# First feed-forward chunk computed token-major, weight tile by weight tile

## The chip, the core and the metric

The kernel runs on one core of a Trainium2 chip. Its time is the device time of one execution in microseconds (us). TensorE (PE) multiplies matrices and transposes, VectorE (DVE) and ScalarE (ACT) work element by element, GpSimd (POOL) does small scalar work, and the queue of SyncE (SP) issues the DMAs. PEld is TensorE's weight load.

## The reference

A two-layer decoder trunk over 256 tokens of width 1024, in float32. A layer is a gated feed-forward part, a token mixer (layer 0 a windowed attention beside a stick-breaking one, layer 1 a dilated attention), a cross-attention into 256 memory tokens, and a second feed-forward part. The change lies in the first feed-forward part of layer 0, with which the program begins:

```python
def swiglu_ffn(x, w_gu, w_down):
    gate, up = jnp.split(x @ w_gu, 2, axis=-1)
    return (jax.nn.silu(gate) * up) @ w_down
x = x + 0.5 * swiglu_ffn(rms_norm(x, ffn1_norm[layer]), ffn1_w_gu[layer], ffn1_w_down[layer])
```

`w_gu` is 1024 x 5632 (gate and up, 2816 columns each), `w_down` 2816 x 1024.

## The kernel before, in words

Every float32 operand of a product is split into two parts: a high part rounded to the format fp32r (a copy on ScalarE) and a low part, what is left (a subtraction on VectorE). A product is then three matmuls: high by high, high by low, low by high (`mm3`, lines 181 to 183). A weight tile is 128 x 1024; `weights` (line 166) loads it into one of four "raw" buffers, makes the high part `wh` (line 174) and the low part `wl` (line 176). There are ten buffers of each of these.

The 2816 hidden features are worked in 11 chunks of 256. A chunk needs 1024 rows of 256 gate and 256 up columns: four weight tiles (`load_chunk`, line 352). The normalised x stands transposed, as 8 blocks of 128 features for each of two token tiles (t = 0, 1) of 128 tokens, in `xs` (high and low). Two forms of a chunk exist:

- feature-major: the weights are the stationary operand, x the moving one, and the result has features on the partitions, as the down projection wants it. `ws_wide` (line 309) does it with matmuls of 512 and 256 columns and sums the two halves; `ws_blocks` (line 293) does it with 256-column matmuls of `mm3`, or pass by pass (`by_pass`, line 300).
- token-major: a block of x is stationary, 512 weight columns (256 gate, 256 up) move, 24 matmuls for a token tile. The result has tokens on the partitions; after silu and product (lines 379 and 380) two transposes (line 385) and a split turn it to features.

In the other three feed-forward parts chunks 0 and 1 are token-major and chunks 2 to 10 go through `ws_wide`. In the first part, before the change, chunk 0 goes through `ws_blocks` with its own tiles (four blocks of 1024 rows x 256 columns, two for gate, two for up), and chunks 1 to 10 through `ws_wide`.

The program starts with `start` (line 327). The gain vector of the first norm, a row in memory, is spread over the partitions by a matmul of ones (line 333). For each token tile `x_updated` makes the square sums (ScalarE, line 213) and `norm_T` the reciprocal root (GpSimd, lines 219 to 222), the scaled x (VectorE, line 226), four transposes for each half (line 207) and the split into `xs` (lines 189 and 190). Then the weight tiles of chunk 0 are split.

What sets the order: the Tile planner orders each engine's instructions by when their operands are ready in its own model of the time, and among ready ones takes the one that stands first in the program. In `start`, `tc.manual_schedule` makes GpSimd, VectorE, ScalarE and TensorE keep the written order of the region's instructions among themselves; SyncE's queue, and where instructions from outside the region fall between them, stay with the planner. `later(delay, fn)` puts work off by a written clock that `tick` advances; `need(tag)` does all that is put off under a tag at once. `announce` (line 232) fetches the norm vector of the next part as a broadcast (line 194) and is called at chunk 2 of the first part.

Of the kernel before, what the change touches and what calls it, by code (L numbers as in the profile page):

```python
# [11 lines left out]
F32 = mybir.dt.float32  # L12
# [26 lines left out]
def kernel(  # L39
# [63 lines left out]
    def tick(ns):  # L103
        clock[0] += ns
        if heap and not busy[0] and heap[0][0] <= clock[0]:
            dispatch()
# [19 lines left out]
    nc.sync.dma_start(row[0:1, :], first_vec.rearrange("(o n) -> o n", o=1))  # L126
    ones = wk.tile([P, 512], F32, name="wk")
    nc.gpsimd.memset(ones[0:1, 0:P], 1.0)
    for t in range(2):
        for c in range(2):  # L130
            cs = slice(c * 512, (c + 1) * 512)
            nc.sync.dma_start(xres[t][:, cs], x_in[0, t * P:(t + 1) * P, cs])
    ident = const.tile([P, P], F32, name="ident")
    make_identity(nc, ident)
    ident_b = const.tile([P, P], BF16, name="ident_b")
# [11 lines left out]
    def psum():  # L147
        return mm.tile([P, 512], F32, name="mm")

    def tps():  # L150
        return tp.tile([P, 512], F32, name="tp")
# [10 lines left out]
    def blocks(ap, n=P):  # L162
        return ap.rearrange("p (a b) -> p a b", b=n)


    def weights(src):
        r = raw.tile([P, 1024], F32, name="raw")
        if len(src.shape) == 4:
            for g in range(2):
                nc.sync.dma_start(r.rearrange("p (k g n) -> p k g n", g=2, n=src.shape[3])[:, :, g, :], src[:, :, g, :])  # L170
        else:
            nc.sync.dma_start(r if len(src.shape) == 2 else blocks(r, src.shape[2]), src)
        wh = wsp.tile([P, 1024], F32R, name="wh")
        nc.scalar.copy(wh, r)  # L174
        wl = wsp.tile([P, 1024], F32R, name="wl")
        nc.vector.tensor_tensor(wl, r, f32(wh), op=ALU.subtract)  # L176
        return wh, wl

    def mm3(ps, a, b, start, stop):

# [21 lines left out]

    def transpose4(src):

        ps = psum() if upcoming.get("starting") else tps()
        for b in range(4):
            nc.tensor.transpose(ps[:, b * P:(b + 1) * P], src[:, b * P:(b + 1) * P], ident)  # L207
        tick(440)
        return ps
# [48 lines left out]
    def xboth(k):  # L258
        return xh[:, :, k, :], xl[:, :, k, :]
# [30 lines left out]
                step(1, c, k, ws[k - head])  # L290
            evac(1, c, ps[1][c])

    def ws_blocks(ps, w, off, per, by_pass=False):

        for b in range(2):
            if by_pass:
                for i, (x, y) in enumerate(((0, 0), (1, 0), (0, 1))):
                    for k in range(NK):
                        o = (k % per) * (1024 // per) + off + b * P
                        nc.tensor.matmul(ps[:, b * 256:(b + 1) * 256], lhsT=w[k // per][x][:, o:o + P],  # L300
                                         rhs=xboth(k)[y], start=i == 0 and k == 0, stop=i == 2 and k == NK - 1)
                        tick(110)
                continue
            for k in range(NK):
                o = (k % per) * (1024 // per) + off + b * P
                mm3(ps[:, b * 256:(b + 1) * 256], cols(w[k // per], o, P), xboth(k), k == 0, k == NK - 1)
                tick(330)
# [16 lines left out]
        return out  # L324


    def start(load):

        et = mybir.EngineType
        with tc.manual_schedule(engines={et.Pool, et.DVE, et.Activation, et.PE}):  # L330
            upcoming["gain"] = [psum(), psum()]
            for c in range(2):
                nc.tensor.matmul(upcoming["gain"][c], lhsT=ones[0:1, 0:P], rhs=row[0:1, c * 512:(c + 1) * 512],
                                 start=True, stop=True)
            for t in range(2):
                for c in range(2):
                    x_updated(t, c)
                clock[0] += 3000.0
            upcoming["starting"] = True
            need("x0")  # L340
            first = load(0)
            need("x1")
            rest = load(1)
            upcoming["starting"] = False
            return first, rest

    def ffn(w_gu, w_down, next_vec, first=False):
        wv = w_gu.rearrange("(k p) n -> p k n", p=P)
        wgu = w_gu.rearrange("(k p) (g n) -> p k g n", p=P, g=2)
        hts = []  # L350

        def load_chunk(c):

            return [weights(wgu[:, 2 * i:2 * i + 2, :, c * 256:(c + 1) * 256]) for i in range(4)]

        def hslot(c):
            if c % 2 == 0:
                hts.append((slot(F32R), slot(F32R)))
            return [blocks(h[:, (c % 2) * 512:(c % 2) * 512 + 512], 256) for h in hts[c // 2]]

        ws = hs = None
        if first:
            f, r = start(lambda i: [weights(wv[:, 0:4, 0:256])] if i == 0 else
                         [weights(wv[:, 4 * (n % 2):4 * (n % 2) + 4, (n // 2) * DFF:(n // 2) * DFF + 256])
                          for n in range(1, 4)])
            ws = [[[f[0], r[0]], r[1:]]]
        else:
            need("x0")
            ws = [load_chunk(0), load_chunk(1)]
            hs = [hslot(0), hslot(1)]  # L370
        for t in range(2):
            need(f"x{t}")
            for c in range(0 if first else 2):
                ps = psum()
                for k in range(NK):
                    mm3(ps, xparts(t, k), cols(ws[c][k // 2], (k % 2) * 512, 512), k == 0, k == NK - 1)
                    tick(650)
                h = work()
                nc.scalar.activation(h[:, 0:256], ps[:, 0:256], AF.Silu)
                nc.vector.tensor_tensor(h[:, 256:512], ps[:, 256:512], h[:, 0:256], op=ALU.mult)  # L380

                def to_features(t=t, c=c, h=h):
                    pst = tps()
                    for b in range(2):
                        nc.tensor.transpose(pst[:, b * P:(b + 1) * P], h[:, 256 + b * P:256 + (b + 1) * P], ident)
                    split_to(hs[c][0][:, :, t * P:(t + 1) * P], hs[c][1][:, :, t * P:(t + 1) * P],
                             blocks(pst[:, 0:256]))
                later(LAG['silu'], to_features)
        if not first:
            announce(next_vec)  # L390
        for c in range(0 if first else 2, NF // 2):
            w = ws[0] if first and c == 0 else load_chunk(c)
            if first and c == 2:
                announce(next_vec)
            if first and c == 0:
                pg = psum()
                ws_blocks(pg, w[0], 0, 4, by_pass=True)
                pu = psum()
                ws_blocks(pu, w[1], 0, 4)
            else:  # L400
                pg = ws_wide(w, 0)
                pu = ws_wide(w, 1)
            s = work()
            nc.scalar.activation(s, pg, AF.Silu)
            h = work()
            nc.vector.tensor_tensor(h, pu, s, op=ALU.mult)
            dh, dl = hslot(c)
            split_to(dh, dl, blocks(h, 256))
        flush()

        def hparts(t, k):
            o = (k % 4) * 256 + t * P
            return hts[k // 4][0][:, o:o + P], hts[k // 4][1][:, o:o + P]

        project(lambda k: w_down[k * P:(k + 1) * P, :], hparts, add_to_x(0.5), nk=NF)
# [101 lines left out]
        return evac  # L517


    def even_mixer(w_in, q_gain, k_gain, sinks, w_out, next_vec, mem, first=False):  # L520
        g = gain_col(q_gain, k_gain, 1, 8.0)
        sink = sm.tile([P, 8], F32, name="sink")
        nc.sync.dma_start(sink, sinks.partition_broadcast(P))
# [90 lines left out]

        nsink = sm.tile([P, 8], F32, name="nsink")
        nc.vector.tensor_scalar(nsink, sink, -1.0, None, op0=ALU.mult)
        if first:
            start(lambda i: None)
        need("x0")
        vb = blocks(slot(), 512)  # L620
        wvb = []
# [321 lines left out]
    for i, (layer, part, _) in enumerate(plan):  # L943
        j = layer // 2
        nxt = plan[i + 1][2][plan[i + 1][0]] if i + 1 < len(plan) else None
        mem = mems[layer]
        cross = (layer, 2) in [p[:2] for p in plan]
        if part == 0:
            ffn(ffn1_w_gu[layer], ffn1_w_down[layer], nxt, first=i == 0)
        elif part == 1 and layer % 2 == 0:  # L950
            even_mixer(ev_w_in[j], ev_q_gain[j], ev_k_gain[j], ev_sinks[j], ev_w_out[j], nxt, mem, first=i == 0)
        elif part == 1:
            odd_mixer(od_w_in[j], od_q_gain[j], od_k_gain[j], od_w_out[j], nxt, mem)
        elif part == 2:
            cross_attention(xa_w_q[layer], xa_q_gain[layer], xa_k_gain[layer], xa_w_o[layer], nxt, mem)
        else:
            ffn(ffn2_w_gu[layer], ffn2_w_down[layer], nxt)
# [56 lines left out]
```

## Time and profile before

| | us |
|---|---|
| median of 3 runs | 1220.24 (1218.81 to 1221.25) |
| the profiled execution | 1220.4 |
| its span, first to last instruction | 1218.6 |
| TensorE busy | 1209.0 (99%) |
| weight load busy | 1023.5 (84%) |
| VectorE busy | 762.2 (63%) |
| ScalarE busy | 648.1 (53%) |
| GpSimd busy | 63.8 (5%) |

All times in rows are microseconds from the span's start. A busy TensorE is not one at its peak: matmuls overlap, and their ends are modelled, so the distance from one start to the next tells the pace. In square brackets stands how long the engine was idle before, and what ended that.

### The profile page before, as it was taken

How to read it: one execution, taken by the hardware profiler on the slowest of the kernel's cores; microseconds unless marked ns; L12 is line 12 of the kernel's file. 1: busy time of each engine (PE TensorE's matmuls, PEld its weight loads, DVE VectorE, ACT ScalarE, POOL GpSimd, SP SyncE). 2: the span in 40 equal slices, each digit the busy share in tenths (PEclk: the TensorE clock that was granted, in tenths of full speed). 3: DMA queues.
4: the chain of work that ended last, by engine and by line, in shares of the span. 5: the costliest groups of instructions: out<-in, count | busy, mean ns of one | idle time of the engine just before them, and what ended most of it. 6: DMA issues, size and time to landing. Idle time of an engine off the chain costs nothing.

```text
span 1218.6 us, 17064 instructions
## 1 busy us (share of the span) xinstructions
PE 1209.0 (99%) x6390; PEld 1023.5 (84%) x6390; DVE 762.2 (63%) x979; ACT 648.1 (53%) x1078; POOL 63.8 (5%) x123
## 2 busy tenths in 40 slices
PE   8999999999999999999999999999999999999998
PEld 7888888887888888888888888888788888888887
DVE  6666645665766676665376675376666776667651
ACT  6656534646655565555365554265643654656540
POOL 1000000200010000000000000033000100000000
PEclk9999999999999999999999999999999999999999
DMA  8765664731444485666385657346634545665560
GB/s 261 248 193 176 220 210 136 257 107 35 138 161 143 141 272 171 195 207 207 104 259 174 207 191 263 117 155 202 204 113 139 189 145 158 222 202 178 182 199 35
DMA packets 136756, 216.71 MB, mean 178 GB/s; under 512 B 10337, under 2 KB 104161, under 8 KB 136674
## 3 DMA queue, kind: packets, MB, share of 16 engines
q1 hardware_dynamic: 136674, 215.63, 54.5%
q8 instruction: 50, 0.82, 0.3%
q14 instruction: 32, 0.26, 0.1%
HBM read 214.54 MB, written 1.05 MB: 177 GB/s over the span
## 4 chain that ended last, share of the span: by engine, by line
PE 95%; DVE 1%; DMA 1%; ACT 1%; issue 0%; POOL 0%; SPq 0%; ACTq 0%; POOLq 0%; DVEq 0%
PE mm L318 22%; PE mm L181 18%; PE mm L182 17%; PE mm L183 17%; PE mm L319 12%; PE tp L207 3%; PE mm L800 1%; DMA raw<-in_xa_w_o_dram 1%; PE mm L821 1%; DVE wl L176 1%; PE mm L582 1%; PE mm L300 1%; DMA x<-in_x_dram 0%; PE mm L603 0%; PE mm L680 0%
## 5 line engine op out<-in xcount | busy, mean ns | idle before, releaser
L176 DVE TENSOR_TENSOR wl<-raw,wh 128x1024 fp32r<-128x1024 f32 x386 | 463.7, 1220 | 145.2 <-ACT wh L174 143.8
L174 ACT CAST wh<-raw 128x1024 fp32r<-128x1024 f32 x386 | 394.0, 1051 | 156.2 <-PE mm L183 80.0
L318 PE MATMUL mm<-xs,wh 128*128 128x512 f32 x1184 | 413.7, 394 | 0.0
L319 PE MATMUL mm<-xs,wl 128*128 128x256 f32 x1184 | 331.8, 280 | 0.0
L318 PEld LDWEIGHTS mm<-xs,wh 128*128 128x128 f32 x1184 | 221.8, 187 | 50.4
L319 PEld LDWEIGHTS mm<-xs,wl 128*128 128x128 f32 x1184 | 223.8, 189 | 0.0
L181 PE MATMUL mm<-wh,big 128*128 128x512 f32 x480 | 193.3, 403 | 0.0
L183 PE MATMUL mm<-wh,big 128*128 128x512 f32 x480 | 187.4, 390 | 0.0
L182 PE MATMUL mm<-wl,big 128*128 128x512 f32 x480 | 187.3, 390 | 0.0
L181 PE MATMUL mm<-wh,xs 128*128 128x512 f32 (+1 forms) x432 | 171.9, 398 | 0.0
L182 PE MATMUL mm<-wl,xs 128*128 128x512 f32 (+1 forms) x432 | 167.6, 388 | 0.0
L183 PE MATMUL mm<-wh,xs 128*128 128x512 f32 (+1 forms) x432 | 167.3, 387 | 0.0
L322 ACT COPY wk<-mm 128x256 f32<-128x256 f32 x148 | 55.3, 374 | 152.0 <-PE mm L319 151.6
L323 DVE TENSOR_TENSOR wk<-mm,wk 128x256 f32<-128x256 f32 x148 | 62.3, 421 | 96.9 <-ACT wk L322 96.9
L181 PEld LDWEIGHTS mm<-wh,big 128*128 128x128 f32 x480 | 90.3, 188 | 19.3 <-issue 2.0
L183 PEld LDWEIGHTS mm<-wh,big 128*128 128x128 f32 x480 | 90.1, 188 | 19.2
L182 PEld LDWEIGHTS mm<-wl,big 128*128 128x128 f32 x480 | 90.4, 188 | 15.9
L183 PEld LDWEIGHTS mm<-wh,xs 128*128 128x128 f32 x432 | 81.2, 188 | 16.5
L181 PEld LDWEIGHTS mm<-wh,xs 128*128 128x128 f32 x432 | 81.3, 188 | 15.2 <-issue 0.3
L182 PEld LDWEIGHTS mm<-wl,xs 128*128 128x128 f32 x432 | 81.4, 188 | 14.3
L207 PE MATMUL tp<-ident,wk 128*128 128x128 f32 x376 | 56.7, 273 | 0.8 <-DVE wk L440 0.8
L207 PEld LDWEIGHTS tp<-ident,wk 128*128 128x128 f32 x376 | 46.0, 141 | 12.4 <-issue 1.6
(159 smaller groups left out, 959.6 us busy)
## 6 DMA issues: line engine op xcount, KB each, us to landing
raw<-in_ffn_w_gu_dram SPq DMA_DIRECT2D x344, 256.0 KB, 4.2
raw<-in_ffn_w_down_dram SPq DMA_DIRECT2D x88, 512.0 KB, 4.4
raw<-in_xa_w_kv_dram SPq DMA_DIRECT2D x32, 512.0 KB, 5.4
raw<-in_od_w_in_dram SPq DMA_DIRECT2D x24, 512.0 KB, 4.4
raw<-in_ev_w_in_dram SPq DMA_DIRECT2D x18, 512.0 KB, 4.5
raw<-in_xa_w_q_dram SPq DMA_DIRECT2D x16, 512.0 KB, 4.6
raw<-in_xa_w_o_dram SPq DMA_DIRECT2D x16, 512.0 KB, 4.3
raw<-in_ev_w_out_dram SPq DMA_DIRECT2D x8, 512.0 KB, 3.8
```

The lines of the kernel that those rows point to most:

```text
L174: nc.scalar.copy(wh, r)
L176: nc.vector.tensor_tensor(wl, r, f32(wh), op=ALU.subtract)
L181: nc.tensor.matmul(ps, lhsT=a[0], rhs=b[0], start=start, stop=False)
L182: nc.tensor.matmul(ps, lhsT=a[0], rhs=b[1], start=False, stop=False)
L183: nc.tensor.matmul(ps, lhsT=a[1], rhs=b[0], start=False, stop=stop)
L207: nc.tensor.transpose(ps[:, b * P:(b + 1) * P], src[:, b * P:(b + 1) * P], ident)
L300: nc.tensor.matmul(ps[:, b * 256:(b + 1) * 256], lhsT=w[k // per][x][:, o:o + P], rhs=xboth(k)[y], start=i == 0 and k == 0, stop=i == 2 an ...
L318: nc.tensor.matmul(ps, lhsT=wh, rhs=xs[:, :, :, k, :], start=k == 0, stop=False)
L319: nc.tensor.matmul(ps[:, 0:256], lhsT=wl, rhs=xh[:, :, k, :], start=False, stop=k == NK - 1)
L322: nc.scalar.copy(part[:, bs], ps[:, 256:512])
L323: nc.vector.tensor_tensor(out[:, bs], ps[:, 0:256], part[:, bs], op=ALU.add)
L582: nc.tensor.matmul(sl, lhsT=qaT[hf * 64:(hf + 1) * 64, b, t * P:(t + 1) * P], rhs=kaT[hf * 64:(hf + 1) * 64, 0:keys], start=False, stop=True)
```

## The change

The first part's chunk 0 becomes token-major. Its tiles are now those of `load_chunk` (256 rows of gate and up columns each), fetched into the "big" buffers, in the order: first half of x, tile 0, second half of x, tiles 1 to 3. `start` computes the chunk tile by tile in a written order: norm of token tile 0, tile 0 for it, norm of token tile 1, tile 1 for token tile 0, transposes of token tile 1, tile 2 for token tile 0, tiles 0 to 2 for token tile 1, then tile 3 for both. Chunk 1 becomes token-major too, as in the other parts. The transposes of the start use the "tp" buffers in PSUM. The vector of the next norm is announced at chunk 3. `weights` is cut into `fetch` and `parts_of`; the `by_pass` form and the mixer's own start, which this program does not use, go.

```diff
-    for t in range(2):
+
+    def load_x(t):
         for c in range(2):
             cs = slice(c * 512, (c + 1) * 512)
             nc.sync.dma_start(xres[t][:, cs], x_in[0, t * P:(t + 1) * P, cs])
+
+    load_x(0)
...
+    def weights(src):
+        return parts_of(fetch(src, raw.tile([P, 1024], F32, name="raw")))
...
-        ps = psum() if upcoming.get("starting") else tps()
+        ps = tps()
...
-    def start(load):
+    def start(first_tiles):
...
-            for t in range(2):
+            raws = [fetch(first_tiles[0], slot())]
+            load_x(1)
+            raws += [fetch(src, slot()) for src in first_tiles[1:]]
+            w, ps = [], [None, None]
+
+            def products(t, i):
+                if i == 0:
+                    ps[t] = psum()
+                for k in (2 * i, 2 * i + 1):
+                    mm3(ps[t], xparts(t, k), cols(w[i], (k % 2) * 512, 512), k == 0, k == NK - 1)
+
+            def normed(t):
                 for c in range(2):
                     x_updated(t, c)
-                clock[0] += 3000.0
-            upcoming["starting"] = True
+
+            normed(0)
             need("x0")
-            first = load(0)
+            w.append(parts_of(raws[0]))
+            products(0, 0)
+            normed(1)
+            w.append(parts_of(raws[1]))
+            products(0, 1)
             need("x1")
-            rest = load(1)
-            upcoming["starting"] = False
-            return first, rest
+            w.append(parts_of(raws[2]))
+            products(0, 2)
+            for i in range(3):
+                products(1, i)
+            w.append(parts_of(raws[3]))
+            products(0, 3)
+            products(1, 3)
+            return w, ps
...
         if first:
-            f, r = start(lambda i: [weights(wv[:, 0:4, 0:256])] if i == 0 else
-                         [weights(wv[:, 4 * (n % 2):4 * (n % 2) + 4, (n // 2) * DFF:(n // 2) * DFF + 256])
-                          for n in range(1, 4)])
-            ws = [[[f[0], r[0]], r[1:]]]
+            w0, done = start([wgu[:, 2 * i:2 * i + 2, :, 0:256] for i in range(4)])
+            ws = [w0, load_chunk(1)]
+            hs = [hslot(0), hslot(1)]
+            for t in range(2):
+                gated(t, 0, done[t])
...
-            for c in range(0 if first else 2):
+            for c in range(1 if first else 0, 2):
...
-        for c in range(0 if first else 2, NF // 2):
-            w = ws[0] if first and c == 0 else load_chunk(c)
-            if first and c == 2:
+        for c in range(2, NF // 2):
+            w = load_chunk(c)
+            if first and c == 3:
                 announce(next_vec)
```

`gated` is the silu, product, transposes and split of lines 378 to 388 before, as a function.

## Rows read from the trace of the kernel before

**Rows 1.** The page: busy time and share by engine; the chain that ended last.

```profile
PE 1209.0 (99%) x6390; PEld 1023.5 (84%) x6390; DVE 762.2 (63%) x979; ACT 648.1 (53%) x1078; POOL 63.8 (5%) x123
...
PE 95%; DVE 1%; DMA 1%; ACT 1%; issue 0%; POOL 0%; SPq 0%; ACTq 0%; POOLq 0%; DVEq 0%
```

**Rows 2.** Chain of waits, 0 to 28 us: start, us, what.

```profile
2.54 5.07 DMA x<-in_x_dram
7.69 0.73 ACT junk L213 x2
...
10.23 1.98 PE mm L207 x8
...
15.89 0.21 PE mm L181
```

**Rows 3.** Timeline of TensorE, 2 to 22 us: start, us, instruction, count, idle before.

```profile
12.02 1.23 PE L300 MATMUL mm<-xs,wh 128*128 128x256 f32 x4
13.82 1.22 PE L300 MATMUL mm<-xs,wh 128*128 128x256 f32 x4 [0.57 <-ACT wh L174]
...
16.97 3.16 PE L300 MATMUL mm<-xs,wh 128*128 128x256 f32 x16
19.97 1.12 PE L300 MATMUL mm<-xs,wl 128*128 128x256 f32 x8
20.92 1.12 PE L300 MATMUL mm<-xs,wh 128*128 128x256 f32 x8
```

**Rows 4.** Stretches: length; busy PE, PEld, DVE, ACT, POOL; PEclk, DMA share, GB/s.

```profile
10.00:12.00 2.00, 1.77 (x8) 1.57 (x8) 2.00 (x5) 1.27 (x2) 0.00 (x0) 1.00 1.11 363
...
18.00:20.00 2.00, 2.00 (x14) 2.00 (x13) 1.26 (x2) 0.64 (x1) 0.00 (x0) 1.00 0.89 272
...
27.40:38.70 11.30, 11.30 (x66) 9.79 (x65) 8.93 (x11) 8.34 (x12) 0.00 (x0) 1.00 0.90 280
```

**Rows 5.** Timeline of ScalarE, 0 to 36 us.

```profile
9.15 0.59 ACT L189 CAST xs<-mm 128x512 fp32r<-128x512 f32 x1 [0.27 <-PE mm L207]
9.63 1.05 ACT L174 CAST wh<-raw 128x1024 fp32r<-128x1024 f32 x1
...
16.93 1.04 ACT L174 CAST wh<-raw 128x1024 fp32r<-128x1024 f32 x1 [1.27 <-DMA raw<-in_ffn_w_gu_dram]
...
22.08 0.60 ACT L404 ACTIVATE wk<-mm 128x512 f32<-128x512 f32 x1 [0.38 <-PE mm L300]
```

**Rows 6.** Timeline of VectorE, 0 to 36 us.

```profile
9.43 1.40 DVE L226 SCALAR_TENSOR_TENSOR wk<-x,rstd,mm 128x512 f32<-128x512 f32 x2 [1.68 <-POOL rstd L222]
...
11.95 1.22 DVE L176 TENSOR_TENSOR wl<-raw,wh 128x1024 fp32r<-128x1024 f32 x1
...
14.28 3.48 DVE L176 TENSOR_TENSOR wl<-raw,wh 128x1024 fp32r<-128x1024 f32 x3
```

**Rows 7.** Timeline of GpSimd, 0 to 20 us.

```profile
4.66 0.22 POOL L219 TENSOR_SCALAR var<-ss 128x1 f32<-128x1 f32 x1 [2.86 <-ACT junk L213]
4.94 0.29 POOL L938 TENSOR_SCALAR_AFFINE_SELECT wk<-wk 128x128 f32<-128x128 f32 x1
```

**Rows 8.** Timeline of SyncE's queue, 0 to 60 us: DMA issues.

```profile
3.01 3.42 SPq L172 DMA_DIRECT2D raw<-in_ffn_w_gu_dram  x4
6.48 1.09 SPq L194 DMA_DIRECT2D gain<-in_mix_norm_dram  x1
```

**Rows 9.** DMA issues, window 3.1 to 3.2 us: count, KB, us to landing.

```profile
raw<-in_ffn_w_gu_dram SPq DMA_DIRECT2D x1, 512.0 KB, 6.0
```

**Rows 10.** Timeline of TensorE around chunk 1, and in the second feed-forward part.

```profile
27.40 0.40 PE L318 MATMUL mm<-xs,wh 128*128 128x512 f32 x1
...
38.72 0.40 PE L318 MATMUL mm<-xs,wh 128*128 128x512 f32 x1
...
439.16 0.38 PE L385 MATMUL tp<-ident,wk 128*128 128x128 f32 x2
...
444.88 0.38 PE L385 MATMUL tp<-ident,wk 128*128 128x128 f32 x2
```

More of the change, by code (lines that the diff above doesn't have):

```diff
@@ L163, in blocks, with fetch @@
         return ap.rearrange("p (a b) -> p a b", b=n)
-    def weights(src):
-        r = raw.tile([P, 1024], F32, name="raw")
+    def fetch(src, r):
         if len(src.shape) == 4:
@@ L172, in weights, with parts_of @@
             nc.sync.dma_start(r if len(src.shape) == 2 else blocks(r, src.shape[2]), src)
+        return r
+    def parts_of(r):
         wh = wsp.tile([P, 1024], F32R, name="wh")
@@ L291, in project, with ws_blocks @@
             evac(1, c, ps[1][c])
-    def ws_blocks(ps, w, off, per, by_pass=False):
+    def ws_blocks(ps, w, off, per):
         for b in range(2):
[L296 to L303, printed above, removed]
             for k in range(NK):
@@ L359, in hslot, with gated, to_features @@
             return [blocks(h[:, (c % 2) * 512:(c % 2) * 512 + 512], 256) for h in hts[c // 2]]
-        ws = hs = None
-        if first:
-            f, r = start(lambda i: [weights(wv[:, 0:4, 0:256])] if i == 0 else
-                         [weights(wv[:, 4 * (n % 2):4 * (n % 2) + 4, (n // 2) * DFF:(n // 2) * DFF + 256])
-                          for n in range(1, 4)])
-            ws = [[[f[0], r[0]], r[1:]]]
+        def gated(t, c, ps):
+            h = work()
+            nc.scalar.activation(h[:, 0:256], ps[:, 0:256], AF.Silu)
+            nc.vector.tensor_tensor(h[:, 256:512], ps[:, 256:512], h[:, 0:256], op=ALU.mult)
+            def to_features():
+                pst = tps()
+                for b in range(2):
+                    nc.tensor.transpose(pst[:, b * P:(b + 1) * P], h[:, 256 + b * P:256 + (b + 1) * P], ident)
+                split_to(hs[c][0][:, :, t * P:(t + 1) * P], hs[c][1][:, :, t * P:(t + 1) * P],
+                         blocks(pst[:, 0:256]))
+            later(LAG['silu'], to_features)
+        if first:
+            w0, done = start([wgu[:, 2 * i:2 * i + 2, :, 0:256] for i in range(4)])
[3 more added lines that the diff above has]
+                gated(t, 0, done[t])
         else:
@@ L377, in ffn @@
                     tick(650)
[L378 to L388, printed above, removed]
+                gated(t, c, ps)
         if not first:
             announce(next_vec)
-        for c in range(0 if first else 2, NF // 2):
-            w = ws[0] if first and c == 0 else load_chunk(c)
-            if first and c == 2:
+        for c in range(2, NF // 2):
+            w = load_chunk(c)
+            if first and c == 3:
                 announce(next_vec)
[L395 to L402, printed above, removed]
+            pg = ws_wide(w, 0)
+            pu = ws_wide(w, 1)
             s = work()
@@ L517, in head256, with even_mixer @@
         return evac
-    def even_mixer(w_in, q_gain, k_gain, sinks, w_out, next_vec, mem, first=False):
+    def even_mixer(w_in, q_gain, k_gain, sinks, w_out, next_vec, mem):
         g = gain_col(q_gain, k_gain, 1, 8.0)
@@ L616, in even_mixer @@
         nc.vector.tensor_scalar(nsink, sink, -1.0, None, op0=ALU.mult)
-        if first:
-            start(lambda i: None)
         need("x0")
@@ L950 @@
         elif part == 1 and layer % 2 == 0:
-            even_mixer(ev_w_in[j], ev_q_gain[j], ev_k_gain[j], ev_sinks[j], ev_w_out[j], nxt, mem, first=i == 0)
+            even_mixer(ev_w_in[j], ev_q_gain[j], ev_k_gain[j], ev_sinks[j], ev_w_out[j], nxt, mem)
         elif part == 1:
```

## The prediction

> **What bounds the kernel now.** I read the page first: TensorE is busy for 1209.0 of the span's 1218.6 us, and the chain of work that ended last is 95% TensorE [rows 1]. The reader is to see there that nothing but TensorE's own queue sets the time once it is running, so a microsecond won or lost before it runs unbroken goes through to the end one for one. The question is therefore only when TensorE gets its unbroken stream, and at what speed.
>
> Then the chain over the first 28 us [rows 2]: the last quarter of x lands at 7.61 (2.54 + 5.07); the square sum, the scale and the eight transposes (1.98 us) of the second token tile follow, and the unbroken stream starts at 13.82, held last by a weight tile's cast [rows 3]. The rows show two speeds: at 15.89 a 256-column product takes 0.21 us of the chain (256 columns in 0.213 us is 1.2 GHz), and the eight that start at 19.97 are followed at 20.92 by the next eight, 0.119 us apart (2.4 GHz) [rows 2, 3]. Between 16.97 and 19.97 sixteen start: twelve at 0.213 and four at 0.119 fill the 3.00 us, so the rise lies near 19.4, after an unbroken stretch since 13.82. The view by stretches writes a granted clock of 1.00 there all the same [rows 4]; the spacing decides.
>
> Chunk 0 ends and chunk 1 starts at 27.40, chunk 2 at 38.72 [rows 10]. **38.72 is the mark**: both versions have done the same work when chunk 2 begins, and all behind it is TensorE-bound.
>
> **Work that is exchanged.** Token-major costs nothing by itself. A run of 24 products of 512 columns with two transposes takes 444.88 − 439.16 = 5.72 us [rows 10]; with a transpose at 0.12 us (half of 1.98 / 8 = 0.247, since these run at the upper speed) a product is 0.228 us. Chunk 1 becomes 2 x 5.72 = 11.44 in place of 38.72 − 27.40 = 11.32; chunk 0 becomes 48 x 0.228 + 4 x 0.12 = 11.4 in place of 96 x 0.119 = 11.4. Sum: +0.1 (bounds ±0.3), which I leave out. On the other engines the silu, the product and the split of two token tiles stand for the sums of partial results; ScalarE is busy for 8.34 and VectorE for 8.93 of chunk 1's 11.30 us [rows 4], so there is room for either form.
>
> **DMAs and the queue.** Four of the tiles go to other buffers than the four "raw" ones, so chunk 1's eight transfers no longer wait for casts; they are issued right behind. The first two transfers of x stay where they are, so the first token tile's chain does not move: its second copy to fp32r starts at 9.15 and the first weight cast at 9.63 [rows 5]. What is fetched after 0.5 MB of x is now weight tile 0, then the second half of x, as the third half megabyte; before, the third half megabyte, issued at 3.01 [rows 8], took 6.0 us and landed at 9.0 [rows 9]. At 363 GB/s [rows 4] every further 524 KB takes 1.45 us: tiles 1 to 3 at 10.5, 11.9, 13.3, chunk 1's at 14.8, 16.2, 17.7, 19.1 (estimates). The norm vector was not fetched at its place even before: it went out at 6.48, in a pause of the queue [rows 8]; it will do so again behind chunk 1's loads, and is wanted only at the end of the part. Cost 0; if it fell in front of chunk 1, its 1.45 us of transfer would lie beside chunk 0's products.
>
> **The order written out, step by step.** The engines keep the region's order, so (us from the span's start):
> - ScalarE: cast of tile 0 9.63 to 10.68 (1.05, [rows 5]); now the two square sums of token tile 1, which ran in an idle time before, at 0.73 each [rows 2]: 12.15; cast of tile 1: 13.2.
> - VectorE: low part of tile 0 12.0 (1.22, [rows 6]). The scale of token tile 1 comes 1.01 us after the squares (8.42 to 9.43, [rows 2, 6]): 13.17; two multiplies 1.40 [rows 6]: 14.57; only then the low part of tile 1: 15.8.
> - TensorE, at 2 x 0.213 = 0.427 per 512 columns: one product of tile 0 at 10.75, five from 12.0 to 14.15; one of tile 1, then a wait to 15.8, five to 17.95. Behind these stand the eight transposes of token tile 1, to 19.93; before, they were over at 12.21 [rows 2]. (That they now use the two "tp" buffers costs 0: token tile 0's splits have left these some 7 us before.)
> - The second copy of token tile 1 ends at 20.5, the cast of tile 2 at 21.55, its low part at 22.8. Before, all four low parts were ready at 17.76 [rows 6].
>
> So the new order starts 1.3 us sooner (10.75 for 12.02, [rows 3]) but its stream breaks twice: 14.6 to 15.8, and from 19.93 to 22.8 with one product in between. What decides is **what fills the second hole**. The region fixes only the order among its own instructions; others may fall between them. The trace shows that for the instruction L938, from outside, which stands on GpSimd between two of the region's [rows 7], and shows that casts are pulled ahead of earlier lines: chunk 1's at 16.93 runs before chunk 0's silu at 22.08 [rows 5]. I take it that chunk 1's casts go into ScalarE's pause after 13.2 (14.8, 16.2, 17.7, 19.1 as they land), its low parts into VectorE's, and its first products (18, for three tiles) into the hole on TensorE. The price on the other side: the cast at 19.1 puts the copies of token tile 1 to 20.2 and tile 2's low part to 23.7; 18 products cover 19.93 to 23.7 at either speed (18 x 0.228 = 4.1 or 18 x 0.427 = 7.7 us).
>
> **The sum.** From 15.8 on TensorE is then unbroken. To the mark it has 96 − 7 = 89 products, eight transposes of x and eight of h. By 19.93: 5 products and the transposes of x. Left: 84 products and 8 x 0.12 = 0.98 us of transposes. If the speed rises at 19.4, as before: 19.9 + 84 x 0.228 + 0.98 = 40.0, +1.3. If it rises as long after the unbroken start as before (5.6 us, 21.4): 3.4 more products at 0.427, the rest at 0.228: 40.7, +2.0. If only at 26: 14 slow ones: 42.9, +4.2. Nothing in the trace says which, since here the stream holds eight transposes in its middle; I take 22.7, between the last two and nearer the one with a row: 6.5 slow products, 77.5 x 0.228 + 0.98: 41.3, **+2.6 us**. On the profiled execution's 1220.4 (span 1218.6 and 1.8 around it) that is **1223.0**; the three runs' median is 1220.24 (1218.81 to 1221.25), so the profile stands for them within 0.2. Against the median it is +0.23%.
>
> **Rivals.**
> - *Hole not filled, speed kept* (B). TensorE waits to 22.8 for tile 2's low part and has by then risen to 2.4 GHz in the stretch 15.8 to 19.93. 35 products of chunk 0, 8.0 us, to 30.85, then chunk 1's 11.44 and chunk 0's transposes 0.49: 42.7, +4.0, 1224.4. For it: the pulled-ahead casts rest on the planner's idea of when chunk 1 lands. Against it: rows 5 and 7.
> - *Hole not filled, slow through it* (C). The array comes out of the tile-by-tile part still at 1.2 GHz, as it was in all of the broken stretch before 13.82, and rises some 3.5 us into the unbroken one at 26.3: 8.1 slow products, 44.3, +5.6, 1226.0. For it: in the trace no rise came before a long unbroken run. The Trainium skill ("TensorE: Matmul & The Clock Gate", section "Loop structure matters more than you think") says this outright: a nest that waits between bursts of one K-tile runs its products cold, one that keeps them back to back does not. By that rule the time would be near 1226; the trace agrees as far as the products up to 15.89, behind the waits, are still 0.21 us apart.
> - *Early rise, not slower* (D). The products at 10.75 and 12.0, with the transposes around them, bring 2.4 GHz before 15.8, and the eight transposes then cost 0.98 in place of 1.98. 89 x 0.228 + 1.96 after 15.8: 38.0, −0.7, 1219.7; with a microsecond's wait for low parts, which VectorE makes at 1.22 each, 1220.7. It decides if products started before 14 count for the rise. Against it: before, eight transposes and four products between 10.23 and 13.25 had not raised it by 15.89 [rows 2, 3]. A gain of more than 2.4 us would need 2.4 GHz from 12.0 and no wait at all: 12.0 + 95 x 0.228 + 1.96 = 35.6, −3.1.
> - *It doesn't do what it says, and the rest moves* (E): the planner orders all later work anew from another start, and a stall of some us comes or goes elsewhere, to either side, 1217 to 1226.
>
> **How the numbers follow.** About 0.2% (2.4 us) is what a measurement of this kernel can tell from no change. The forecast (filled hole, +1.3 to +4.2) has 0.42, B 0.14, C 0.12, D 0.22, E 0.10. Above 1222.7 lie 0.23 of the forecast's 0.42, B, C and 0.03 of E: slower 0.52. Within: 0.19 of the forecast, 0.18 of D, 0.02 of E: same 0.39. Faster: 0.04 of D, 0.05 of E: 0.09. The range reaches from D's lower edge to just past C's time: 1218.8 to 1226.6; the forecast's own is 1221.5 to 1224.5.
>
> **What would show it.** Right: the low part of tile 1 ends near 15.8 and that of tile 2 near 22.8 to 23.7, behind token tile 1's scale and copies; the transposes of token tile 1 end near 20 and not 12.2; products of chunk 1 stand between them and tile 2's; chunk 2 starts near 41.3. Wrong: chunk 2 starts at 38.7 or before; or tile 1's low part comes before the scale of token tile 1; or 512-column products are 0.228 us apart at 15.8 (D); or no chunk 1 product stands ahead of tile 2's (B, C); or the difference is made after chunk 2's start (E).

## The result and the profile after

The changed kernel takes 1227.03 us (median of 7 runs, 1223.52 to 1227.89), the kernel before in the same runs 1219.94 (1217.21 to 1222.55). The ratio is 1.0051, interval 1.0034 to 1.0068: slower by about 6.2 us (so far apart are the means; the medians are 7.1 apart). The direction was forecast. The size was not: the forecast of 1223.0 (+2.6 us) and its own range to 1224.5 lie below. On the forecast's base of 1220.24 the ratio gives 1226.5, just inside the whole range, whose end of 1226.6 was set for rival C and not for the forecast. Of the ways that were written down, rival C is the nearest to what came: the hole stays empty, and the array runs slow behind it.

The page of the kernel after, the lines that answer to [rows 1]: TensorE is as busy as before, only over a longer span, so its busy time shows nothing; the page's first slice of 30 us does, with 7 tenths of TensorE's time for 8 before.

```profile
PE 1211.0 (99%) x6334; PEld 1020.6 (83%) x6334; DVE 761.4 (62%) x979; ACT 646.7 (53%) x1078; POOL 64.1 (5%) x123
...
PE   7999999999999999999999999999999999999998
...
PE 94%; DMA 3%; DVE 2%; ACT 1%; SPq 0%; issue 0%; POOL 0%; ACTq 0%; POOLq 0%; DVEq 0%
```

TensorE's timeline of the kernel after (start, us, instruction, idle before), to be read against [rows 3]:

```profile
10.66 0.79 PE L189 MATMUL mm<-wh,xs 128*128 128x512 f32 x1 [1.62 <-ACT wh L179]
11.92 0.80 PE L190 MATMUL mm<-wl,xs 128*128 128x512 f32 x1 [0.47 <-DVE wl L181]
...
15.60 0.80 PE L190 MATMUL mm<-wl,xs 128*128 128x512 f32 x1 [0.75 <-DVE wl L181]
...
17.90 1.81 PE L215 MATMUL tp<-ident,wk 128*128 128x128 f32 x8
21.33 0.50 PE L189 MATMUL mm<-wh,xs 128*128 128x512 f32 x1 [1.62 <-ACT wh L179]
22.59 0.56 PE L190 MATMUL mm<-wl,xs 128*128 128x512 f32 x1 [0.76 <-DVE wl L181]
...
43.77 0.48 PE L318 MATMUL mm<-xs,wh 128*128 128x512 f32 x1
...
55.28 0.40 PE L318 MATMUL mm<-xs,wh 128*128 128x512 f32 x1
```

The stream breaks twice for low parts, before 15.60 and before 22.59, as forecast, and between the transposes and 22.59 stands one product alone: this is the hole. Chunk 2 starts at 43.77 where it started at 38.72 [rows 10]: +5.05 us.

VectorE and ScalarE of the kernel after show who made the hole [rows 5, 6 before]:

```profile
13.00 1.41 DVE L234 SCALAR_TENSOR_TENSOR wk<-x,rstd,mm 128x512 f32<-128x512 f32 x2 [1.14 <-DMA raw<-in_ffn_w_gu_dram]
14.33 1.22 DVE L181 TENSOR_TENSOR wl<-big,wh 128x1024 fp32r<-128x1024 f32 x1
19.61 1.45 DVE L198 TENSOR_TENSOR xs<-tp,xs 128x512 fp32r<-128x512 f32 x2 [4.07 <-ACT xs L197]
21.31 2.36 DVE L181 TENSOR_TENSOR wl<-big,wh 128x1024 fp32r<-128x1024 f32 x2 [0.25 <-DMA gb<-in_ev_k_gain_dram]
```

```profile
11.89 1.03 ACT L179 CAST wh<-big 128x1024 fp32r<-128x1024 f32 x1
18.99 0.59 ACT L197 CAST xs<-tp 128x512 fp32r<-128x512 f32 x1 [6.07 <-PE tp L215]
19.75 0.59 ACT L197 CAST xs<-tp 128x512 fp32r<-128x512 f32 x1 [0.17 <-PE tp L215]
20.23 1.99 ACT L179 CAST wh<-big 128x1024 fp32r<-128x1024 f32 x2
22.12 3.88 ACT L179 CAST wh<-raw 128x1024 fp32r<-128x1024 f32 x4
```

ScalarE stands idle for 6.07 us before 18.99. Chunk 1's tiles had begun to land in that time (its eight half-tile transfers were issued from 8.32 on, 6.0 us each), but their four casts run only at 22.12, behind tile 3's. The reader should not follow the releaser in the last line of VectorE: a vector of the mixer is named because it landed last, at 21.2; the cast of tile 2, which ended at 21.26 (20.23 + 1.03), is what tile 2's low part waited for. The chain of waits of this kernel runs into the same DMA, which is a part of why its page shows DMA at 3%.

The view by stretches of the kernel after (length; busy PE, PEld, DVE, ACT, POOL; granted clock, DMA share, GB/s):

```profile
15.60:19.40 3.80, 3.80 (x13) 3.21 (x13) 0.00 (x0) 0.41 (x1) 0.00 (x0) 1.00 1.01 330
19.50:22.80 3.30, 0.92 (x4) 0.40 (x3) 2.87 (x4) 3.13 (x5) 0.00 (x0) 1.00 0.39 81
22.90:26.30 3.40, 3.40 (x9) 2.64 (x8) 3.40 (x4) 3.11 (x4) 0.00 (x0) 0.50 0.11 20
26.40:30.00 3.60, 3.60 (x18) 2.97 (x17) 2.45 (x5) 1.57 (x2) 0.00 (x0) 1.00 0.91 283
```

In the hole TensorE is busy for 0.92 of 3.30 us; right behind it the granted clock is 0.50 (1.2 GHz) for 3.4 us in which TensorE is busy all the time, nine products where the next 3.6 us hold eighteen. The 1.00 of the first row tells nothing of the clock: the view writes it ahead of the first rise too, and the products there start 0.427 us apart (16.19, 16.62, 17.05), which is 1.2 GHz. The array had risen to 2.4 GHz by 21.33: the product there, behind a wait, shows 0.50 us where the one at 15.60, behind a wait too, shows 0.80. So the hole cost its own length and then the speed.

Of the rest of the difference, 0.2 us are the two transposes in chunk 2 (chunk 3 starts at 55.28, 5.27 later than before). Some 1.0 us more come before the second feed-forward part (its chunk 2 starts at 457.05, and at 450.74 before), where ScalarE waits 2.81 us for a tile, with the next norm's squares queued behind it. The first line is of the kernel before, the other two of the kernel after:

```profile
428.63 1.06 ACT L174 CAST wh<-raw 128x1024 fp32r<-128x1024 f32 x1 [1.55 <-DMA raw<-in_ffn_w_gu_dram]
```

```profile
435.12 1.05 ACT L179 CAST wh<-raw 128x1024 fp32r<-128x1024 f32 x1 [2.81 <-DMA raw<-in_ffn_w_gu_dram]
436.08 0.62 ACT L221 ACTIVATE junk<-x 128x512 bf16<-128x512 f32 x1
```

5.05 + 0.2 + 1.0 is 6.3 of the 6.5 us between the two spans. Only the 5.05 us at the mark can come from the written order of `start`: e1_norms_first, which undoes that order, has the longer wait before the second feed-forward part as well.

### The profile page after: what moved, and what is told of

Its sections match the earlier page's. It is cut to its first block, busy times and chain, and to the rows that moved or that the text cites. A ratio compares the mean times of both kernels' runs of the same rounds, so it can differ in the third digit from the quotient of the medians.

```text
span 1225.1 us, 16958 instructions
## 1 busy us (share of the span) xinstructions
PE 1211.0 (99%) x6334; PEld 1020.6 (83%) x6334; DVE 761.4 (62%) x979; ACT 646.7 (53%) x1078; POOL 64.1 (5%) x123
## 4 chain that ended last, share of the span: by engine, by line
PE 94%; DMA 3%; DVE 2%; ACT 1%; SPq 0%; issue 0%; POOL 0%; ACTq 0%; POOLq 0%; DVEq 0%
PE mm L318 22%; PE mm L189 18%; PE mm L190 17%; PE mm L191 17%; PE mm L319 11%; PE tp L215 3%; PE mm L816 1%; DVE wl L181 1%; DMA raw<-in_xa_w_o_dram 1%; PE mm L837 1%; DMA raw<-in_ffn_w_gu_dram 1%; PE mm L600 1%; DMA big<-in_ffn_w_gu_dram 1%; PE mm L621 0%; PE mm L696 0%
## 5 line engine op out<-in xcount | busy, mean ns | idle before, releaser
L181 DVE TENSOR_TENSOR wl<-raw,wh 128x1024 fp32r<-128x1024 f32 x382 | 458.8, 1220 | 143.1 <-ACT wh L179 141.7
L179 ACT CAST wh<-raw 128x1024 fp32r<-128x1024 f32 x382 | 389.9, 1051 | 153.9 <-PE mm L191 79.5
L318 PE MATMUL mm<-xs,wh 128*128 128x512 f32 x1152 | 402.5, 394 | 0.0
L319 PE MATMUL mm<-xs,wl 128*128 128x256 f32 x1152 | 322.8, 280 | 0.0
L318 PEld LDWEIGHTS mm<-xs,wh 128*128 128x128 f32 x1152 | 215.7, 187 | 48.8
L319 PEld LDWEIGHTS mm<-xs,wl 128*128 128x128 f32 x1152 | 217.7, 189 | 0.0
L189 PE MATMUL mm<-wh,xs 128*128 128x512 f32 (+1 forms) x464 | 186.3, 402 | 3.2 <-ACT wh L179 3.2
L190 PE MATMUL mm<-wl,xs 128*128 128x512 f32 (+1 forms) x464 | 181.9, 392 | 2.0 <-DVE wl L181 2.0
L191 PE MATMUL mm<-wh,xs 128*128 128x512 f32 (+1 forms) x464 | 181.4, 391 | 0.0
L189 PEld LDWEIGHTS mm<-wh,xs 128*128 128x128 f32 x464 | 88.2, 190 | 20.5 <-ACT wh L179 3.9
L190 PEld LDWEIGHTS mm<-wl,xs 128*128 128x128 f32 x464 | 88.3, 190 | 19.2 <-DVE wl L181 3.5
L191 PEld LDWEIGHTS mm<-wh,xs 128*128 128x128 f32 x464 | 88.1, 190 | 17.9
```

Source lines behind the costliest of these rows:

```text
L189: nc.tensor.matmul(ps, lhsT=a[0], rhs=b[0], start=start, stop=False)
L190: nc.tensor.matmul(ps, lhsT=a[0], rhs=b[1], start=False, stop=False)
L191: nc.tensor.matmul(ps, lhsT=a[1], rhs=b[0], start=False, stop=stop)
L318: nc.tensor.matmul(ps, lhsT=wh, rhs=xs[:, :, :, k, :], start=k == 0, stop=False)
L319: nc.tensor.matmul(ps[:, 0:256], lhsT=wl, rhs=xh[:, :, k, :], start=False, stop=k == NK - 1)
```

## The experiments

Theory W: the written order of `start` costs the time, by its waits and by the speed that the waits cost. Rival F: the token-major form and the moved loads cost it. Two narrower rivals stand with their runs: G for the late announcement, L for the order of the loads. Each line: the ratio to the kernel before in the same runs, and the start of chunk 2 in the profiled execution.

| run | ratio to before | interval | chunk 2 at, us |
|---|---|---|---|
| kernel before | 1 | | 38.72 |
| changed | 1.0051 | 1.0034 to 1.0068 | 43.77 |
| e9_changed_again | 1.0050 | 1.0033 to 1.0067 | 43.76 |
| e2_announce_2 | 1.0042 | 1.0027 to 1.0058 | 44.70 |
| e6_x_whole_first | 1.0042 | 1.0029 to 1.0055 | 42.24 |
| e4_filler | 1.0021 | 1.0011 to 1.0032 | 42.50 |
| e5_chunk1_in_hole | 1.0016 | 1.0006 to 1.0027 | 39.81 |
| e3_hole_filled | 1.0009 | 1.0000 to 1.0017 | 38.66 |
| e8_chunk1_form | 1.0001 | 0.9992 to 1.0009 | 39.17 |
| e1_norms_first | 0.9987 | 0.9978 to 0.9996 | 37.43 |
| e7_norms_first_mm | 0.9984 | 0.9975 to 0.9993 | 38.03 |

**The whole order undone, the form kept (e1_norms_first).**

```diff
-            raws = [fetch(first_tiles[0], slot())]
-            load_x(1)
+            load_x(1)
+            raws = [fetch(first_tiles[0], slot())]
...
             normed(0)
+            clock[0] += 3000.0
+            normed(1)
             need("x0")
             w.append(parts_of(raws[0]))
-            products(0, 0)
-            normed(1)
-            w.append(parts_of(raws[1]))
-            products(0, 1)
             need("x1")
...
+            w += [parts_of(r) for r in raws[1:]]
+            for i in range(4):
+                products(0, i)
+                products(1, i)
```

> The changed kernel with the preparation in the order of the kernel before: x loaded whole ahead of the weight tiles, both norms and both sets of transposes ahead of the later tiles' parts, then the token-major products tile by tile for both token tiles. Theory W (the loss comes from the written order: token tile 1's norm and transposes between the tiles): the low parts are ready by 17.8 us as before, the stream is unbroken from about 13.2, chunk 2 starts at 38.7 +- 1, time within 1.5 us of the kernel before. Rival F (the token-major form, its eight transposes and the moved loads cost the time): it stays 4 to 6 us above the kernel before.

Ratio 0.9987: the whole loss is gone, and 1.6 us more. Chunk 2 starts at 37.43, a little ahead of what was expected; the products are 0.23 us apart from 17.04 on, so the speed rose some 2 us sooner than in the trace of the kernel before. VectorE of this kernel shows that all four low parts are over by 18.56 (expected: 17.8), and that token tile 1's scale is back in its idle time at 9.43:

```profile
9.43 1.41 DVE L234 SCALAR_TENSOR_TENSOR wk<-x,rstd,mm 128x512 f32<-128x512 f32 x2 [1.67 <-POOL rstd L230]
...
11.95 1.22 DVE L181 TENSOR_TENSOR wl<-big,wh 128x1024 fp32r<-128x1024 f32 x1
...
15.06 3.50 DVE L181 TENSOR_TENSOR wl<-big,wh 128x1024 fp32r<-128x1024 f32 x3 [0.25 <-ACT wh L179]
```

Chunk 0 and chunk 1 are token-major here, the tiles go by the big buffers, the announcement is the late one: rival F falls.

**The announcement (e2_announce_2).** `if first and c == 2` for `c == 3`, nothing else.

> The changed kernel with the next norm vector announced at chunk 2 again. Theory W: no difference to the changed kernel (within 1 us; some 5 to 7 us above the kernel before), the fetch goes out in a pause of the queue in both. Rival G (the late fetch delays something): 1 us or more is won back.

Ratio 1.0042; its interval holds the changed kernel's ratio. Rival G finds no support. This execution's mark is the latest of all, 44.70: here the array did not rise before the hole, and the products went on at 0.427 us to 27.8.

**The hole filled with chunk 0's own work (e3_hole_filled).**

```diff
             products(0, 1)
-            need("x1")
-            w.append(parts_of(raws[2]))
+            w += [parts_of(r) for r in raws[2:]]
             products(0, 2)
-            for i in range(3):
-                products(1, i)
-            w.append(parts_of(raws[3]))
+            need("x1")
             products(0, 3)
-            products(1, 3)
+            for i in range(4):
+                products(1, i)
```

> The changed kernel with one change of order: the parts of tiles 2 and 3 come before token tile 1's transposes, and the product of tile 2 for token tile 0 stands ahead of them, that of tile 3 behind. Theory W with the second hole as its larger part: TensorE runs unbroken from 15.6, the speed rises near 19.4 and does not fall back, chunk 2 starts near 39.6 in place of 43.8: 4 us faster than the changed kernel, about 1 us above the kernel before. Rival F: no gain over the changed kernel beyond 1 us.

Ratio 1.0009: 0.42% or 5.1 us of the loss come back by this one change of order, with the first wait (to 15.69) left as it is. What still divides it from e1_norms_first, 0.22% or 2.7 us, is the rest of the order, the first wait among it; no run takes that apart. On TensorE of this kernel the transposes stand between products and the longest wait behind them is 0.51 us:

```profile
15.69 0.50 PE L190 MATMUL mm<-wl,xs 128*128 128x512 f32 x1 [0.75 <-DVE wl L181]
...
18.34 1.03 PE L215 MATMUL tp<-ident,wk 128*128 128x128 f32 x8
19.13 0.47 PE L189 MATMUL mm<-wh,xs 128*128 128x512 f32 x1
...
21.27 0.50 PE L189 MATMUL mm<-wh,xs 128*128 128x512 f32 x1 [0.51 <-ACT xs L197]
```

Its mark, 38.66, flatters it by the early rise of that execution (products 0.23 us apart from 16.03 on; 39.6 was expected); the ratio is over 11 runs. ScalarE and VectorE of this kernel show chunk 1's casts, as its tiles land, and two of its low parts ahead of token tile 1's copies at 20.64 and 21.25:

```profile
15.24 1.05 ACT L179 CAST wh<-raw 128x1024 fp32r<-128x1024 f32 x1 [0.33 <-DMA raw<-in_ffn_w_gu_dram]
...
17.82 2.36 DVE L181 TENSOR_TENSOR wl<-raw,wh 128x1024 fp32r<-128x1024 f32 x2
```

**The hole filled with work that is no use (e4_filler).** Twelve matmuls into a PSUM tile of their own, behind token tile 1's transposes:

```diff
             need("x1")
+            spare = psum()
+            for n in range(12):
+                nc.tensor.matmul(spare, lhsT=xh[:, 0, n % 4, :], rhs=w[0][0][:, 0:512], start=n == 0, stop=n == 11)
             w.append(parts_of(raws[2]))
```

> The changed kernel with twelve matmuls of 512 columns into a spare PSUM tile that nobody reads, behind token tile 1's transposes: the hole stays as long as it is for all useful work, but TensorE is busy in it. If the fall of the clock at 22.9 us is a part of the loss by itself: no fall, the 8 to 9 slow products from 22.6 to 26.3 take 0.227 in place of 0.427, chunk 2 starts near 42.0 in place of 43.8, 1.7 us faster than the changed kernel. If the wait alone is the loss: no difference.

The first products behind the filler, and the stretches of this kernel, the second at the same time as above:

```profile
22.83 0.39 PE L189 MATMUL mm<-wh,xs 128*128 128x512 f32 x1
23.06 0.39 PE L190 MATMUL mm<-wl,xs 128*128 128x512 f32 x1
...
20.80:22.80 2.00, 2.00 (x10) 1.64 (x9) 1.75 (x3) 2.00 (x3) 0.00 (x0) 1.00 0.27 40
22.90:26.30 3.40, 3.40 (x17) 2.81 (x16) 3.40 (x4) 3.12 (x4) 0.00 (x0) 1.00 0.10 14
```

The clock does not fall, and seventeen products stand in the stretch that held nine. The mark is 1.27 us earlier for 1.7 expected; the filler ran over, so that the second product, at 22.59 without it, comes at 23.06, 0.47 later. The fall therefore cost 1.27 + 0.47 = 1.7 us in the trace of the changed kernel. By the ratios 0.30% or 3.6 us come back. The two numbers differ, and a part of that can be named: the wait of 2.81 us before the second feed-forward part is 1.66 in this kernel's trace. So the fall by itself is worth 1.7 us in this pair of executions; what it is worth on the mean over runs, these ratios do not take apart from the rest.

**The forecast's condition by hand (e5_chunk1_in_hole).** Chunk 1's first two tiles and their twelve products for token tile 0 are written into the hole:

```diff
             products(0, 1)
+            ahead = [weights(next_tile(i)) for i in range(2)]
             need("x1")
+            pn = psum()
+            for k in range(4):
+                mm3(pn, xparts(0, k), cols(ahead[k // 2], (k % 2) * 512, 512), k == 0, False)
             w.append(parts_of(raws[2]))
...
```

> The changed kernel with the forecast's condition written out by hand: the parts of chunk 1's tiles 0 and 1 come behind tile 1's, and their twelve products for token tile 0 stand between token tile 1's transposes and tile 2's product. Theory W: TensorE has useful work in the hole, chunk 2 starts at 40 to 41.5 us, the time is 1.3 to 2.6 us above the kernel before, 3.5 to 5 below the changed one. Rival (the price is elsewhere, the hole only shows it): no gain over the changed kernel.

Ratio 1.0016 (+2.0 us), between the bounds that the forecast had set for this case, +1.3 and +4.2, and near its +2.6. The sum, however, was made for the mark, and there the trace shows less: 39.81, +1.09 us, a little ahead of the 40 to 41.5 expected; with the speed rising near 20.5, as it did here, the sum would give some +1.7. The rest of the time is made behind the mark (the span is 3.9 us longer than before). ScalarE of this kernel shows the casts in the pause, 0.4 us behind the times that the prediction had put the tiles' landing at (14.8 and 16.2):

```profile
15.19 1.05 ACT L179 CAST wh<-raw 128x1024 fp32r<-128x1024 f32 x1 [2.21 <-DMA raw<-in_ffn_w_gu_dram]
16.63 1.05 ACT L179 CAST wh<-raw 128x1024 fp32r<-128x1024 f32 x1 [0.40 <-DMA raw<-in_ffn_w_gu_dram]
19.04 0.59 ACT L197 CAST xs<-tp 128x512 fp32r<-128x512 f32 x1 [1.36 <-PE tp L215]
```

**The loads' order undone, the written order kept (e6_x_whole_first).** Only the two lines of the first diff's head (`load_x(1)` ahead of tile 0).

> The changed kernel with both halves of x loaded ahead of weight tile 0, as before, the written order kept. Theory W: token tile 1's squares wait for ScalarE's cast of tile 0 and not for x, so nothing changes: within 1 us of the changed kernel, tile 1's low part still ends near 15.6 and tile 2's near 22.5. Rival L (the order of the loads holds token tile 1 up): 2 us or more are won back.

Ratio 1.0042, not to be told from the changed kernel's; tile 1's low part ends at 15.7 as before. Rival L falls. Tile 2's came sooner than expected, at 20.9, because in this execution the array had risen by 15 and the products and transposes ahead of it ran at 2.4 GHz. That brought the mark 1.5 us forward, to 42.24, and no more: the clock fell all the same, behind a shorter hole.

```profile
15.00:21.60 6.60, 3.40 (x18) 2.47 (x17) 3.88 (x5) 3.90 (x6) 0.00 (x0) 1.00 0.86 273
21.80:25.00 3.20, 3.20 (x9) 2.43 (x9) 3.20 (x4) 2.64 (x3) 0.00 (x0) 0.50 0.23 41
```

**Norms first, transposes in the larger pool (e7_norms_first_mm).** e1 with `ps = psum() if upcoming.get("starting") else tps()` in `transpose4`, set around the two `need` calls.

> The kernel with both norms first (e1_norms_first), with the start's transposes in the six-buffer PSUM pool again, as before the change. In e1_norms_first token tile 1's transposes waited from 9.1 to 11.5 us for VectorE to clear the two tp buffers; here they should start at 10.2 as before, and the products about 0.5 to 0.9 us sooner. Expected: 0 to 1 us faster than e1_norms_first, 1 to 2.5 us faster than the kernel before. If the first low part (VectorE) holds the products anyway: no difference to e1_norms_first.

Ratio 0.9984. The transposes do start sooner (9.84 for 11.49), and the first product too, but the second waits for the first low part, so little of it is left; against e1 the difference is not resolved.

```profile
9.84 1.97 PE L215 MATMUL mm<-ident,wk 128*128 128x128 f32 x8 [0.77 <-DVE wk L234]
11.46 0.78 PE L189 MATMUL mm<-wh,xs 128*128 128x512 f32 x1
12.83 0.79 PE L190 MATMUL mm<-wl,xs 128*128 128x512 f32 x1 [0.59 <-DVE wl L181]
```

Both kernels with the norms first beat the kernel before, by 1.6 and 2.0 us, at the edge of what can be told.

**The form alone (e8_chunk1_form).** The kernel before with chunk 1 token-major behind chunk 0:

```diff
-            for c in range(0 if first else 2):
+            for c in range(1 if first else 0, 2):
...
-        for c in range(0 if first else 2, NF // 2):
+        for c in range(2, NF // 2):
...
```

> The kernel before with chunk 1 alone made token-major, behind chunk 0 as it was. Theory W and the sum of the prediction: the form costs 0.1 us in chunk 1 and two transposes (0.2 us) in chunk 2, so within 0.5 us of the kernel before. Rival F (the form costs the time): 3 us or more above it.

Ratio 1.0001: the form of chunk 1 costs nothing that can be measured, as the sum had it; for chunk 0 e1_norms_first shows the same.

**The changed kernel once more (e9_changed_again).** No edit but a comment.

> The changed kernel as it is, once more. Theory W: the written order gives the same waits in every execution (tile 1's low part to 15.6, tile 2's to 22.5), and what varies is where TensorE's clock rises and whether it falls again in the hole; so the low parts stand within 0.3 us of the first trace, chunk 2 starts between 42 and 45 us, and the times spread over some 4 us, more than the kernel before. If the waits vary as well, the low parts move by 1 us or more.

Ratio 1.0050. VectorE of this execution has the same waits within 0.15 us, and the clock falls again behind the hole:

```profile
14.21 1.22 DVE L181 TENSOR_TENSOR wl<-big,wh 128x1024 fp32r<-128x1024 f32 x1
...
21.29 2.36 DVE L181 TENSOR_TENSOR wl<-big,wh 128x1024 fp32r<-128x1024 f32 x2 [0.25 <-ACT wh L179]
```

```profile
19.80:23.20 3.40, 1.13 (x4) 0.73 (x5) 2.98 (x4) 3.40 (x5) 0.00 (x0) 1.00 0.35 61
23.30:26.60 3.30, 3.30 (x10) 2.53 (x9) 3.30 (x4) 2.69 (x3) 0.00 (x0) 0.50 0.14 31
```

That the times would spread more than those of the kernel before did not come true: 1225.6 to 1228.8 here, 1217.8 to 1224.2 there in the same runs. The wait before the second feed-forward part is there again too, 2.84 us. It does not belong to the written order: every trace of a kernel with chunk 0 token-major has it at 2.4 to 3.0 us, e1_norms_first (2.44, the line below) and e3_hole_filled (3.03) too, but for e4_filler (1.66); the kernel before and e8_chunk1_form have 1.55 and 1.62. Its cause stays open.

```profile
428.55 1.05 ACT L179 CAST wh<-raw 128x1024 fp32r<-128x1024 f32 x1 [2.44 <-DMA raw<-in_ffn_w_gu_dram]
```

## Why the prediction was right or wrong, by its steps

- *What bounds the kernel* held in the main: 5.05 us at chunk 2 are 6.5 at the end. "One for one" is too strong: set against the trace of the kernel before, the traces of the experiments change their distance by −1.2 us (e4_filler) to +2.9 us (e5_chunk1_in_hole) between the mark and the end.
- *Exchanged work* held: +0.1 us was summed, e8_chunk1_form shows a ratio of 1.0001.
- *DMAs and the queue* held: the norm vector's place (e2_announce_2) and the order of the loads (e6_x_whole_first) make no difference that can be measured. Chunk 1's transfers did not go out at once behind the others, but some 0.75 us apart from 8.32 to 13.9; its tiles were there near the forecast times all the same (the first two casts in e5_chunk1_in_hole at 15.19 and 16.63 for 14.8 and 16.2).
- *The written order, step by step* held to 0.3 us: first product 10.75 forecast and 10.66 measured, second 12.0 and 11.92, tile 1's products 15.8 and 15.60, transposes over 19.93 and 19.7, tile 2's cast from 20.5 and 20.23, its products 22.8 and 22.59. A queue that keeps its order can be worked out from the rows of the kernel before.
- *"I take it that chunk 1's casts go into ScalarE's pause"* failed. It is the step on which the size hung: the pause of 6.07 us stayed empty, no product of chunk 1 stood in the hole, and the mark came 5.05 us late for the +2.6 forecast. The two rows behind it (an outside instruction between two of the region's, casts ahead of an earlier silu) show that the planner may do so, not that it would. e5_chunk1_in_hole shows that the sum was near for the case it assumed (+1.09 at the mark where it gives +1.7), and that the case had to be written by hand. Why the planner left the pause empty stays open; that it places work by its own model of the time, in which the pause need not exist, is likely and not shown. In e3_hole_filled it did put chunk 1's casts and two of its low parts ahead of token tile 1's copies, so it is not the region that forbids it.
- *The speed.* Rival C put the unfilled hole with a slow array at chunk 2 at 44.3; it came at 43.77 and 43.76 in two executions of the changed kernel and at 44.70 in e2_announce_2. In the last the array had not risen before the hole, as C had it. In the other two it had risen and fell behind the hole, which no rival had; that C's price fits them is luck, since its slow stretch (22.8 to 26.3, the 3.5 us being in no row of the kernel before) is by chance the one in which the array was slow again (22.9 to 26.3). So the range held the measured ratio by a rival's bound and not by the forecast's working. The rule that was weighed with C (the Trainium skill, "TensorE: Matmul & The Clock Gate", section "Loop structure matters more than you think": a long wait between matmuls lets them run cold, matmuls back to back stay warm) was the better guide here than the planner's reordering, though the waits here are 1.62 and 0.76 us with a product between; e4_filler agrees with it, since there the speed stays up although the useful work waits as long as before.
- *Early rise* (D) was possible but not the case that counts: e6_x_whole_first had it, and its time is not to be told from the changed kernel's.
- *The rest of the program moved* (E) by 1.0 us, with one wait before the second feed-forward part; the other kernels with chunk 0 token-major, but for e4_filler, have it too, so it is not the written order's.

## What to carry to other kernels

Where an order is written out for engines that keep it, write down for each engine the whole list with the durations of the old trace before trusting it: here one norm placed between two weight tiles put the low part of tile 2 at 22.5 us, where the kernel before had all four by 17.8, and the list showed it to 0.3 us. Do not count on a planner to fill a hole because it may; put independent work into it by hand, or take out what makes it. A hole in TensorE's stream can be dearer than it is long, since the clock can fall behind it (1.7 us here).

## What the runs showed of the hardware

- The rise to 2.4 GHz came anywhere from 15 to 28 us in the eleven profiled executions of nearly the same start, and the fall behind the hole was seen in three of the four executions that had the hole empty (the fourth had not risen). With the hole empty the start of chunk 2 moved with it, from 42.24 to 44.70. The whole times of the changed kernel spread no more for it than those of the kernel before: 1223.5 to 1228.8 in 13 runs, 1217.2 to 1224.2 in the 18 of the kernel before beside them.
- The chunks 3 to 10 of the first part, made of pairs of 512 and 256 columns, have two paces at a granted clock of 1.00. Two executions of the changed program, the first trace and e9_changed_again, show it; the rows are the same chunk, in stretches of its length (the next one starts at 66.59 and at 66.34):

```profile
55.30:66.60 11.30, 11.30 (x67) 9.79 (x66) 7.29 (x11) 6.38 (x11) 0.00 (x0) 1.00 0.61 188
```

```profile
55.25:66.34 11.09, 11.09 (x66) 9.78 (x65) 7.29 (x11) 6.36 (x11) 0.00 (x0) 1.00 0.63 191
```

Eight chunks at 11.31 or 11.09 us differ by 1.8 us with no other sign in the profile. Six of the eleven traces, the kernel before among them, have the slower pace. So two profiled executions should be compared by marks ahead of that stretch, and their ends only with 2 us of doubt.
